# Quarter 0's head queries: behind quarter 2's keys and values instead of behind quarter 0's, from inputs kept in DRAM

## The chip, the core and the metric

One core of a Trainium2 chip runs the whole kernel. The metric is the device time in microseconds (us) of one execution, as the median of several runs. The engines are TensorE (PE; PEld are its weight loads), VectorE (DVE), ScalarE (ACT), GpSimd (POOL) and SyncE (SP, which issues most loads); each has its own queue of instructions, taken in order. ACT's queue also issues the stores.

## The reference

One decoder layer over 2048 tokens of width 1024, in float32: sparse attention with a top-256 indexer, then a SwiGLU network, each followed by a layer norm.

```
proj = h @ w_in                      # q | c_kv | q_idx | k_idx | w_idx
c_kv = rms_norm(c_kv, kv_norm_g)
q_lat = einsum('blhd,hcd->blhc', q, w_uk) * HEAD_DIM ** -0.5
rel   = relu(einsum('bqhd,bsd->bqhs', q_idx, k_idx))
score = einsum('bqh,bqhs->bqs', w_idx, rel)            # causal, else -inf
sel   = top_k(score, 256)
logits = einsum('bqhc,bqkc->bhqk', q_lat, c_kv[sel]) - slope * distance
o_lat  = einsum('bhqk,bqkc->bqhc', softmax(logits), c_kv[sel])
o = einsum('blhc,hcd->blhd', o_lat, w_uv) @ w_o
x = layer_norm(alpha * x + o);  x = layer_norm(alpha * x + swiglu_ffn(x))
```

The change touches only where `q`, the heads' part of the projection, is computed for the first 512 tokens.

## The kernel before

The tokens are worked on in four quarters of 512 (four blocks of 128 each). Until the attention starts, the program is a list of steps in `ORDER`, each a letter and a quarter:

- `i` (`index_part`, then `scores`): transposes the quarter of x on TensorE into 8 tiles of 128x512, each as a high and a low float32r part (tags `xh`, `xl`, `XB` = 8 buffers of each); projects index keys, index queries and the latent (the last matmuls are 264 columns wide); then computes the index scores of its blocks: per head two or more matmuls (L360), a ReLU on ACT (L362) and a weighted addition into the block's score row `S` on DVE (L365, L367).
- `k` (`kv_part`): keys and values of the quarter from the latent, stored to DRAM (`ks`, `vs`).
- `h` (`heads_part`): the heads' queries, eight tiles of 24 matmuls of 512 columns, one weight load and one split of it into two parts on POOL (L188, L159) for each; stored to DRAM as `qs`.
- `w` prepares the weights of `k`; `f` finishes the selection of blocks 2 to 7.

Every product of float32 values is three float32r matmuls (L234 to L236). Behind each `i` step stands the top-256 search of its blocks (`topk_near`): nine rounds in which a threshold is moved by a count, on DVE (L436 to L441) for two blocks and on ACT (L446 to L448) for the other two. It has a low priority: a scheduler, which orders each engine's instructions by priority and by its own model of time, puts it where it thinks there is room. `topk_rest` then reads one flag on DVE (L515 to L520) and branches at L521 (`tc.If`, an exact search that these inputs do not need). All engines take that branch, so it is a gate in every queue. There are two: one for blocks 2 to 7, one for blocks 8 to 15, the second called from the attention over the first 1024 tokens. Behind it `select` turns the scores into masks on DVE and ACT (L535 to L545).

`heads_part` takes its 8 pairs of input tiles either as they are left from the `i` step of its quarter (quarters 0 and 3 here), or loads them again from the DRAM tensor `xs`, to which `transposed` wrote them (`spill`, quarters 1 and 2 here). The attention follows the last `h` step: logits (L629), mask and row minimum on DVE (L630), exponentials on ACT (L635), transposes (L657) and their copies (L659), values (L668).

Of the kernel before, what the change touches and what calls it, by code (L numbers as in the profile page):

```python
# [46 lines left out]
XB = 8  # L47
# [3 lines left out]
NEV, NRL, NRAW = 3, 2, 2  # L51
NHI, NLO = 2, 2
NCS = 4
ORDER = "i0 w0 k0 h0 i1 k1 i2 f0 k2 i3 k3 h3 h2 h1".split()
ROUNDS = 9
BITS = {0: ([2], [3]), 1: ([4, 5], [6, 7]), 2: ([8, 9], [10, 11]), 3: ([12, 13], [14, 15])}

# [18 lines left out]
def trunk(tc, x, w_in, w_uk, w_uv, kv_g, w_o, w_gu, w_down, lm_g, lm_b, lf_g, lf_b, out, stop=99):  # L76
# [64 lines left out]
    xs = dram.tile([NQUART, KT, 2, P, QUART], F32, name="xs")  # L141
# [111 lines left out]
    def later():  # L253

        return at(tc.cur_priority + 1000000)
# [39 lines left out]
    def index_part(pp, pq, pe, bk, st, t):  # L295

        t0 = t * QUART
        tok = slice(t0, t0 + QUART)
        n0 = 8 if t == 1 else 12
        xx = transposed(pp, bk, "x", x, t0, XB, nat=[S[b] for b in range(n0, n0 + 4)], spill=xs[t] if t in (1, 2) else None)  # L300
        xh, xl = xx
        kst = st["kst"]

# [67 lines left out]
    def heads_part(pp, pe, bk, t, xx):  # L371

        t0 = t * QUART
        tok = slice(t0, t0 + QUART)
        if xx is None:
            xx = reloaded(pp, "x", xs[t], XB)
        for j in range(NPAIR):
            o = proj_tile(pp, bk, xx, [(lambda v: v, w3[:, :, j * P:(j + 1) * P])])
            evac(pe, o, 0.125, qs[j], tok)
# [781 lines left out]
    S = {}  # L1161
# [14 lines left out]
    with Banks("psb", big=(2, 2)) as big:  # L1176
        pe = pool("pe")
        pp = pool("pp")
        pq = pool("pq", "right")
        with Banks("psp", tp=(2, 1), mm=(2, 1)) as sml:  # L1180
            bk = lambda tag: big("big") if tag == "sc" else sml(tag)
# [3 lines left out]
            done = {}  # L1185
            for what, t in ((o[0], int(o[1])) for o in ORDER):
                if what == "i":
                    done[t] = index_part(pp, pq, pe, bk, st, t)
                    for b in range(max(2, t * BPQ), (t + 1) * BPQ):
                        scores(pq, bk, st, b)  # L1190
                    with later():
                        topk_near(tk, *BITS[t])
                elif what == "f":
                    with later():
                        topk_rest(tk, ((2, 2), (4, 4)))
                elif what == "w":
                    kv_weights()
                elif what == "k":
                    kv_part(pp, pe, bk, st, t)
                else:  # L1200
                    heads_part(pp, pe, bk, t, done[t] if t in (0, 3) else None)
        close("pq", "pp")
        ak = pool("ak", "right")
        ap = pool("ap", "right")
# [1 line left out]
        with Banks("psa", tp=(3, 1), oc=(1, 1)) as sml:  # L1206
            bk = lambda tag: big("big") if tag == "mm" else sml(tag)
# [61 lines left out]
```

## Time and profile before

| | us |
|---|---|
| median of 3 runs (lowest, highest) | 3155.91 (3154.04, 3174.88) |
| the profiled execution | 3164.37 |
| its span, first to last instruction | 3162.6 |
| TensorE busy in the span | 2963.8 |

In the trace, `mm`, `big`, `tp` and `oc` are tiles that TensorE writes, `wraw`, `whi` and `wlo` a weight and its two parts, `sm` a tile of logits or probabilities, `rl` the ReLU of scores. A busy time is the union of an engine's instructions. A wait is idle time of an engine, put down to what released it. A row "a <- b" of waits says that a waited for b.

### The profile page before, as it was taken

What the parts mean: (1) busy time and instruction counts of PE and PEld (TensorE: products, weight loads), DVE (VectorE), ACT (ScalarE), POOL (GpSimd) and SP (SyncE); (2) the same over time, 40 slices, a digit from 0 to 9 for tenths busy, and PEclk for the clock granted to TensorE, in tenths of its full rate; (3) what the DMA queues carried; (4) which work ended last, traced back from release to release, by engine and by line L of the source; (5) the groups of instructions that cost most, each with busy time, mean ns of one, the idle gap of its engine ahead of it and who ended that gap; (6) DMA issues with size and microseconds to landing.
All of it is one profiled execution on the core that took longest, in us unless ns stands there. A gap on an engine that the chain in (4) does not pass through costs nothing.

```text
span 3162.6 us, 44469 instructions
## 1 busy us (share of the span) xinstructions
PE 2963.8 (94%) x15067; PEld 2303.2 (73%) x15067; DVE 1918.4 (61%) x2904; ACT 1541.2 (49%) x2913; POOL 1557.1 (49%) x1342
## 2 busy tenths in 40 slices
PE   7988899887899999999999989999899999999996
PEld 5776677665566776676777768888678888878875
DVE  3436869977954544655556675555865555245299
ACT  2434858459877777666632233333333333333333
POOL 4433143452543334333336366666776666645475
PEclk9999999998899999999999979999899999999998
DMA  9777655573346756776559443223233222755353
GB/s 291 227 211 227 194 166 176 176 226 94 110 124 173 188 150 158 191 181 171 142 155 267 149 145 109 100 100 104 99 131 107 100 100 87 233 170 170 107 162 138
DMA packets 460728, 498.98 MB, mean 158 GB/s; under 512 B 51408, under 2 KB 332112, under 8 KB 460496
## 3 DMA queue, kind: packets, MB, share of 16 engines
q1 hardware_dynamic: 369280, 359.09, 40.4%
q10 hardware_dynamic: 91216, 137.01, 12.2%
q8 instruction: 120, 1.97, 0.3%
q14 instruction: 112, 0.92, 0.1%
HBM read 359.01 MB, written 136.97 MB: 157 GB/s over the span
## 4 chain that ended last, share of the span: by engine, by line
PE 63%; DVE 9%; DMA 4%; ACT 3%; issue 2%; SPq 1%; POOL 0%; ACTq 0%; DVEq 0%; POOLq 0%
PE mm L234 9%; PE mm L236 9%; PE mm L235 9%; PE oc L668 8%; PE tp L657 8%; PE big L629 7%; PE mm L1056 3%; PE mm L1054 3%; PE mm L1055 3%; DVE cl L159 1%; PE mm L837 1%; PE mm L838 1%; PE mm L839 1%; DVE hx L872 1%; DMA inv<-rsd 1%
## 5 line engine op out<-in xcount | busy, mean ns | idle before, releaser
L618 POOL TENSOR_SCALAR sm<-S 128x768 f32<-128x768 f32 (+7 forms) x384 | 339.7, 892 | 527.7 <-PE tp L657 473.9
L234 PE MATMUL mm<-ch,wh 128*128 128x512 f32 x1232 | 492.3, 401 | 16.5 <-ACT ch L867 13.6
L235 PE MATMUL mm<-cl,wh 128*128 128x512 f32 x1232 | 485.9, 395 | 6.6 <-DVE cl L159 5.7
L236 PE MATMUL mm<-ch,wl 128*128 128x512 f32 x1232 | 489.1, 397 | 0.0
L630 DVE CUSTOM_DVE_ANT_0 sm<-big,sm 128x1024 f32<-128x1024 f32 (+7 forms) x256 | 232.6, 922 | 247.6 <-PE big L629 203.2
L659 ACT COPY pt<-tp 128x512 f32<-128x512 f32 (+1 forms) x524 | 274.3, 559 | 181.3 <-PE tp L657 179.0
L635 ACT ACTIVATE sm<-sm,mx 128x768 f32<-128x768 f32 (+7 forms) x384 | 343.8, 899 | 23.9 <-DVE mx L630 23.5
L657 PE MATMUL tp<-ident,sm 128*128 128x128 f32 x2176 | 312.6, 284 | 27.5 <-ACT sm L635 17.2
L159 POOL TENSOR_TENSOR wl<-s,wh 128x512 fp32r<-128x512 f32 x176 | 238.4, 1360 | 194.9 <-ACT wh L920 194.9
L657 PEld LDWEIGHTS tp<-ident,sm 128*128 128x128 f32 x2176 | 236.5, 142 | 132.8 <-issue 97.5
L234 PEld LDWEIGHTS mm<-ch,wh 128*128 128x128 f32 x1232 | 235.3, 191 | 68.3 <-ACT ch L867 17.8
L235 PEld LDWEIGHTS mm<-cl,wh 128*128 128x128 f32 x1232 | 235.1, 191 | 64.0 <-DVE cl L159 9.8
L236 PEld LDWEIGHTS mm<-ch,wl 128*128 128x128 f32 x1232 | 235.4, 191 | 54.7
L920 ACT CAST wh<-s 128x512 fp32r<-128x512 f32 x176 | 109.0, 621 | 332.9 <-DVE s L909 91.4
L629 PE MATMUL big<-kka,aqd 128*128 128x512 f32 (+3 forms) x896 | 232.3, 387 | 25.2 <-DVE mx L630 19.6
L159 POOL TENSOR_TENSOR wl<-wr,wh 128x512 fp32r<-128x512 f32 x132 | 190.0, 1440 | 97.5 <-ACT wh L920 96.0
L159 POOL TENSOR_TENSOR cl<-hx,ch 128x512 fp32r<-128x512 f32 (+2 forms) x106 | 152.8, 1445 | 157.2 <-ACT ch L1049 136.2
L367 DVE SCALAR_TENSOR_TENSOR S<-rl,wi,S 128x768 f32<-128x768 f32 (+5 forms) x161 | 177.8, 1122 | 82.4 <-ACT rl L362 77.5
L668 PE MATMUL oc<-pt,vva 128*64 128x256 f32 (+1 forms) x1536 | 206.5, 390 | 0.8 <-DVE ot L672 0.8
L1049 ACT CAST ch<-hx 128x512 fp32r<-128x512 f32 (+2 forms) x158 | 94.8, 610 | 217.4 <-PE tp L1055 96.9
L362 ACT ACTIVATE rl<-big 128x768 f32<-128x768 f32 (+5 forms) x184 | 141.6, 790 | 118.5 <-PE big L360 57.2
L188 POOL TENSOR_SCALAR whi<-wraw 128x1024 fp32r<-128x1024 f32 (+1 forms) x60 | 72.6, 1211 | 253.8 <-PE mm L235 118.7
(296 smaller groups left out, 6556.1 us busy)
## 6 DMA issues: line engine op xcount, KB each, us to landing
wr<-in_f_w_gu SPq DMA_DIRECT2D x44, 1024.0 KB, 5.2
gs<-cc ACTq DMA_DIRECT2D x154, 256.0 KB, 2.0
hx<-gs SPq DMA_DIRECT2D x144, 256.0 KB, 2.9
aqd<-qs SPq DMA_DIRECT2D x256, 128.0 KB, 3.6
wraw<-in_a_w_in SPq DMA_DIRECT2D x56, 512.0 KB, 4.1
kka<-ks SPq DMA_DIRECT2D x96, 256.0 KB, 4.4
hx<-in_f_w_down SPq DMA_DIRECT2D x66, 256.0 KB, 3.0
qd<-qis SPq DMA_DIRECT2D x112, 128.0 KB, 4.5
```

The costliest lines, as they stand in the source:

```text
L159: (eng or nc.vector).tensor_tensor(out=lo, in0=src, in1=f(hi), op=ALU.subtract)
L234: nc.tensor.matmul(o, lhsT=lh, rhs=rh, start=(i == 0), stop=False)
L235: nc.tensor.matmul(o, lhsT=lh, rhs=rl, start=False, stop=False)
L236: nc.tensor.matmul(o, lhsT=ll, rhs=rh, start=False, stop=(i == n - 1))
L367: nc.vector.scalar_tensor_tensor(sv, rl[:, :wn], wi[:, h:h + 1], sv, op0=ALU.mult, op1=ALU.add)
L618: nc.gpsimd.tensor_scalar(out=sm[:, :wn], in0=S[b0 + i][:, w0:w0 + wn], scalar1=slope, scalar2=1.0, op0=ALU.mult, op1=ALU.mult)
L629: pe(nc.tensor.matmul(o[:, s0:s0 + n], lhsT=qd[:, c, i * P:(i + 1) * P], rhs=kk[wi_][e][:, s0:s0 + n], start=(c == 0), stop=(c == 1)))
L630: nc.vector.tensor_tensor_reduce(out=sm[:, :wn], in0=o, in1=sm[:, :wn], scale=-1.0, scalar=mx[:, i, 0:1] if wi_ else 3.0e38, op0=ALU.add, ...
L635: nc.scalar.activation(sm[:, :n], sm[:, :n], AF.Exp, bias=mx[:, i_, nw - 1:nw], scale=-1.0, accum_out=su[:, i_, e, w_:w_ + 1])
L657: pe(nc.tensor.transpose(tp[:, at:at + P], self.prob(e, i, kb), ident))
L659: pcopy(pt[:, :2 * n], tp[:, :2 * n])
L668: pe(nc.tensor.matmul(self.ob[e * HD:(e + 1) * HD, i0 * P:256], lhsT=self.vv[kb][:, e * HD:(e + 1) * HD], rhs=pt[:, e * n:(e + 1) * n], st ...
```

## The change

`h0` moves in `ORDER` from behind `k0` to behind `k2`. By then the input tiles of quarter 0 have been overwritten by those of quarters 1 and 2, so `transposed` now writes them to `xs` in `i0` as well, and `heads_part` loads them again.

```diff
@@ -51,7 +51,7 @@
 NEV, NRL, NRAW = 3, 2, 2
 NHI, NLO = 2, 2
 NCS = 4
-ORDER = "i0 w0 k0 h0 i1 k1 i2 f0 k2 i3 k3 h3 h2 h1".split()
+ORDER = "i0 w0 k0 i1 k1 i2 f0 k2 h0 i3 k3 h3 h2 h1".split()
 ROUNDS = 9
 BITS = {0: ([2], [3]), 1: ([4, 5], [6, 7]), 2: ([8, 9], [10, 11]), 3: ([12, 13], [14, 15])}
 
@@ -297,7 +297,7 @@
         t0 = t * QUART
         tok = slice(t0, t0 + QUART)
         n0 = 8 if t == 1 else 12
-        xx = transposed(pp, bk, "x", x, t0, XB, nat=[S[b] for b in range(n0, n0 + 4)], spill=xs[t] if t in (1, 2) else None)
+        xx = transposed(pp, bk, "x", x, t0, XB, nat=[S[b] for b in range(n0, n0 + 4)], spill=xs[t] if t < 3 else None)
         xh, xl = xx
         kst = st["kst"]
 
@@ -1198,7 +1198,7 @@
                 elif what == "k":
                     kv_part(pp, pe, bk, st, t)
                 else:
-                    heads_part(pp, pe, bk, t, done[t] if t in (0, 3) else None)
+                    heads_part(pp, pe, bk, t, done[t] if t == 3 else None)
         close("pq", "pp")
         ak = pool("ak", "right")
         ap = pool("ap", "right")
```

The scheduler lays out every engine's queue anew. At the start of ACT's queue, where the transposed tiles of quarter 0 are made (`xh`, `xl` their two parts, `S` here the staging for the weights of `w`, `kh` the index keys), stood before:

```order
L210 CAST xh<-tp 128x512 x8
L268 CAST S_171<-S_169 128x1024
L270 DMA wkv<-S_171 128x1024
L271 DMA wkv<-S_172 128x1024
L307 CAST kh<-mm 128x512
```

and stands now:

```order
L210 CAST xh<-tp 128x512 x2
L213 DMA xs<-xh 128x512 x2
L214 DMA xs<-xl 128x512 x2
L210 CAST xh<-tp 128x512 x2
L213 DMA xs<-xh 128x512 x2
L214 DMA xs<-xl 128x512 x2
L210 CAST xh<-tp 128x512
L213 DMA xs<-xh 128x512
```

Eight more such stores follow among the last casts and the first stores of `wkv`; they are new in this place.

On PE, right behind the last tile of `k0` (`cth`, `ctl` are the latent's two parts), stood the first tile of `h0`, on the tiles that `i0` left:

```order
L234 MATMUL mm_1130<-whi_1096,cth_503 128x512
L235 MATMUL mm_1130<-wlo_1097,cth_503 128x512
L236 MATMUL mm_1130<-whi_1096,ctl_504 128x512
L234 MATMUL mm_1146<-xh_234,whi_1141 128x512
L235 MATMUL mm_1146<-xl_235,whi_1141 128x512
```

Now `i1` follows there, and `h0` stands behind `k2`, on tiles that were loaded again (`xh_4482` and so on), with score matmuls of the third quarter's blocks between its own:

```order
L234 MATMUL mm_4578<-xh_4482,whi_4573 128x512
L235 MATMUL mm_4578<-xl_4483,whi_4573 128x512
L236 MATMUL mm_4578<-xh_4482,wlo_4574 128x512
L360 MATMUL big_3146<-kst_207,qd_3099 128x512 x2
L360 MATMUL big_3146<-kst_207,qd_3099 128x384 x2
L360 MATMUL big_3154<-kst_207,qd_3099 128x512 x2
L234 MATMUL mm_4578<-xh_4486,whi_4573 128x512
L235 MATMUL mm_4578<-xl_4487,whi_4573 128x512
```

On PE at the second gate (L521) stood before, with 252 matmuls of the attention ahead of it:

```order
L629 MATMUL big<-kka,aqd 128x512 x4
L668 MATMUL oc<-pt,vva 64x256 x2
L668 MATMUL oc<-pt,vva 64x128 x2
L657 MATMUL tp<-ident,sm 128x128 x4
L521 UNCONDITIONAL_BRANCH
L657 MATMUL tp<-ident,sm 128x128 x4
```

(the trace records each L668 as two, so that it has some 300 records there), and now, with 25:

```order
L236 MATMUL mm<-xh,wlo 128x512
L629 MATMUL big<-kka,aqd 128x128 x2
L629 MATMUL big<-kka,aqd 128x256 x2
L657 MATMUL tp<-ident,sm 128x128 x6
L629 MATMUL big<-kka,aqd 128x384 x2
L629 MATMUL big<-kka,aqd 128x512 x2
L629 MATMUL big<-kka,aqd 128x384 x2
L629 MATMUL big<-kka,aqd 128x512 x2
L657 MATMUL tp<-ident,sm 128x128 x3
L521 UNCONDITIONAL_BRANCH
```

The last head matmul (`mm<-xh,wlo`) now stands just ahead of the gate. Behind it both orders have the same attention. Counted the same way, 384 score matmuls stand ahead of the last 264-wide latent matmul of quarter 3, where 324 stood. From the end of quarter 3's latent projection to the second gate DVE has 50 score additions (62 before), 22 counts and 22 threshold steps of the search (36 and 36) and 8 mask-and-minimum pieces (30), ACT 60 ReLUs (75), 27 sign counts (36), 8 exponentials (30) and 2 copies of transposes (28).

## Rows read from the trace of the kernel before

**Rows 1.** The page's busy time by engine over the whole span.

```profile
PE 2963.8 (94%) x15067; PEld 2303.2 (73%) x15067; DVE 1918.4 (61%) x2904; ACT 1541.2 (49%) x2913; POOL 1557.1 (49%) x1342
```

**Rows 2.** Busy time by stage; last columns: granted clock, DMA share, GB/s.

```profile
0.00:79.00 79.00, 58.30 (x272) 46.18 (x272) 27.22 (x38) 20.72 (x41) 36.17 (x85) 0.92 1.00 291
79.00:114.00 35.00, 31.03 (x122) 23.00 (x122) 23.65 (x56) 19.88 (x44) 5.61 (x9) 0.93 0.82 250
114.00:158.00 44.00, 44.00 (x193) 36.01 (x192) 11.33 (x21) 14.24 (x34) 27.95 (x16) 1.00 0.68 209
290.00:395.00 105.00, 93.01 (x455) 74.92 (x454) 85.56 (x155) 76.24 (x168) 31.81 (x33) 0.95 0.60 179
395.00:447.00 52.00, 52.00 (x280) 45.00 (x279) 25.12 (x27) 19.31 (x34) 24.28 (x16) 1.00 0.54 148
704.00:784.00 80.00, 54.90 (x305) 37.56 (x304) 64.14 (x122) 75.33 (x151) 27.67 (x38) 0.83 0.30 87
1027.00:1185.00 158.00, 157.19 (x1130) 111.96 (x1131) 76.48 (x177) 121.02 (x265) 58.33 (x77) 1.00 0.64 169
447.00:784.00 337.00, 285.28 (x1288) 220.02 (x1286) 287.49 (x386) 239.11 (x412) 136.68 (x112) 0.94 0.56 171
```

**Rows 3.** Waits of TensorE, 704 to 784: total us, times, longest.

```profile
PE tp L657 <- ACT sm L635: 13.4, 10, 3.1
PE big L629 <- DVE mx L630: 5.8, 5, 1.7
```

**Rows 4.** Timeline of VectorE at the gate: start, duration in us.

```profile
780.30 0.14 DVE L519 TENSOR_SCALAR worsti<-all 1x1 int32<-1x1 f32 x1
784.15 1.09 DVE L630 CUSTOM_DVE_ANT_0 sm<-big,sm 128x896 f32<-128x896 f32 x1 [3.71 <-DVEq L521]
```

**Rows 5.** Line 234: durations in ns (min/median/max), first and last start.

```profile
L234 PE MATMUL mm<-whi,xh x128: 278/283/425, 53.6 to 446.4; 128*128 128x264 f32 x128
```

**Rows 6.** DMA issues, 0 to 1000 us: KB each, us to landing.

```profile
xs<-xh ACTq DMA_DIRECT2D x16, 256.0 KB, 4.7
xh<-xs SPq DMA_DIRECT2D x16, 256.0 KB, 5.1
```

**Rows 7.** Line 367, then timelines of VectorE and POOL near 590 us.

```profile
L367 DVE SCALAR_TENSOR_TENSOR S<-rl,wi,S x161: 474/1020/3418, 69.6 to 675.3; 128x768 f32<-128x768 f32 x42, 128x896 f32<-128x896 f32 x42, 128x1024 f32<-128x1024 f32 x28, 128x384 f32<-128x384 f32 x21
590.92 3.33 DVE L367 SCALAR_TENSOR_TENSOR S<-rl,wi,S 128x896 f32<-128x896 f32 x1
590.96 5.51 POOL L159 TENSOR_TENSOR wlo<-wraw,whi 128x1024 fp32r<-128x1024 f32 x2
```

**Rows 8.** Groups of ScalarE, 447 to 784: busy us, mean ns, idle.

```profile
L362 ACT ACTIVATE rl<-big 128x1024 f32<-128x1024 f32 (+2 forms) x76 | 69.5, 926 | 52.0 <-DVE S L367 13.4 <-PE big L360 10.3 <-PE mm L236 9.6
L446 ACT ACTIVATE ja<-S,t 128x1408 int8<-128x1408 f32 (+3 forms) x36 | 62.5, 1737 | 1.1 <-POOL t L423 1.1
L635 ACT ACTIVATE sm<-sm,mx 128x128 f32<-128x128 f32 (+7 forms) x30 | 23.0, 771 | 1.5 <-DVE mx L630 1.5
L659 ACT COPY pt<-tp 128x512 f32<-128x512 f32 (+1 forms) x28 | 14.3, 559 | 1.6 <-PE tp L657 1.4
```

**Rows 9.** Groups of VectorE, 447 to 784, in the same columns.

```profile
L367 DVE SCALAR_TENSOR_TENSOR S<-rl,wi,S 128x1024 f32<-128x1024 f32 (+2 forms) x68 | 92.6, 1379 | 22.6 <-ACT rl L362 19.3 <-DVEq L521 3.1
L436 DVE TENSOR_SCALAR_CACHE_REDUCE jv<-S,t 128x1152 int8<-128x1152 f32 (+3 forms) x36 | 62.6, 1740 | 2.7 <-POOL t L423 2.5
L630 DVE CUSTOM_DVE_ANT_0 sm<-big,sm 128x128 f32<-128x128 f32 (+7 forms) x30 | 20.9, 725 | 9.2 <-PE big L629 9.1
L441 DVE SCALAR_TENSOR_TENSOR t<-g,st,t 128x1 f32<-128x1 f32 x36 | 10.4, 329 | 0.4
```

**Rows 10.** Groups of TensorE, 690 to 784, the attention's three lines.

```profile
L629 PE MATMUL big<-kka,aqd 128*128 128x512 f32 (+3 forms) x96 | 26.3, 413 | 5.8 <-DVE mx L630 5.8
L657 PE MATMUL tp<-ident,sm 128*128 128x128 f32 x108 | 21.2, 324 | 19.3 <-ACT sm L635 13.4 <-ACT pt L659 5.7
L668 PE MATMUL oc<-pt,vva 128*64 128x256 f32 (+1 forms) x104 | 13.4, 381 | 0.0
```

## The prediction

> **What bounds the kernel now.** I read the page's head first, then the busy time by stage, then the waits of TensorE in the one stage that stands out, then the groups of instructions there. Over the span TensorE is busy 94% [rows 1], so most of the 3162.6 us is matmuls that this change only carries from one place to another. The stages [rows 2] show where time is lost. From 0 to 79 us the sixteen DMA engines are busy all of the time (share 1.00, 291 GB/s) and TensorE 58.3 of 79 us. From 114 to 158 TensorE is busy throughout: these are the 192 matmuls of step h0, the heads' queries of quarter 0. VectorE is busy 85.6 of 105 us between 290 and 395. The worst stage is 704 to 784: TensorE 54.9 of 80 us at a granted clock of 0.83, while ScalarE is busy 75.3 us. There the first pairs of the attention run beside the last top-k search, and TensorE waits for the exponentials and for the row minima [rows 3]. At the end of that stage stands the second gate, the branch at L521 that every engine takes when VectorE knows whether the last blocks need the exact search: VectorE reads the flag at 780.3 us and goes on at 784.15, after a wait of 3.71 us [rows 4]. I call 784 the time of the gate. After the attention has settled, TensorE is busy 157.2 of 158 us with 1130 matmul records, 0.140 us each [rows 2].
>
> So the change is worth what it does to two dates: when the gate opens, and how much attention stands before it.
>
> **The change part by part.** All dates are of the profiled execution. I carry them from the end of quarter 3's latent projection, whose last matmul starts at 446.4 us [rows 5], to the gate.
>
> Spill of quarter 0's transposed inputs: 16 DMAs of 256 KB, 4.19 MB, on ScalarE's queue among the casts of the first 30 us. Such a store lands after a median of 4.7 us where the kernel has them already [rows 6]. The place is the stage with DMA share 1.00. Bounds: nothing, if the loads that TensorE waits for overtake; 4.19 MB / 291 GB/s = 14.4 us, if all of it goes ahead of them. Nothing is idle on the DMA side, so I stay near the upper end: 12 us.
>
> h0 leaves 114 to 158: 192 matmuls at 44.0 us / 193 = 0.228 us [rows 2], about 44 us, and everything from i1 to k2 comes 44 us earlier. Quarter 1's own 32 DMAs for inputs and spill (4.19 MB of it stores) now fall into k0, where the share is 0.82 of 35 us, so 6 us are free and 8 of 14.4 us are not [rows 2]. Bounds 0 and 14.4; TensorE has other work in k0, so I take 4 us. That quarter 1's transposes no longer wait for h0's buffers, and quarter 3's now do, I set against each other at zero.
>
> h0 comes back behind k2: the same 44 us, so this pair cancels. The 16 reloads (4.19 MB, 5.1 us each to land [rows 6]) run while k2 computes, at a share of 0.54 to 0.60 [rows 2], and cost nothing; without that cover 14.4 us. SP's queue issues them between the weights and the queries of the scores, and each of the others there waits only behind issues. But h0 stands among the scores of blocks 8 to 11 now, on a VectorE that was 81% busy. Its eight weight splits run on POOL: 16 instructions, 27.95 us between 114 and 158 [rows 2], 3.5 us for a split. One score addition that began beside such splits took 3.33 us, where the median of all 161 is 1.02 [rows 7]. Low end nothing (TensorE has h0's own matmuls to do), high end 8 x 3.5 us = 28 us if each split held one addition for its whole length. The 68 additions of the later stretch, with as many splits beside them, took a mean of 1.379 us [rows 9], some 0.36 us over that median, so I take a microsecond for each split: 8 us.
>
> Here the Trainium skill speaks against the change: "SBUF — State Buffer", section "Who interferes with whom", says that a VectorE instruction with two inputs in SBUF contends with a GpSimd instruction that reads SBUF, and that whoever is second is blocked until the first is done. By that rule the term would be the 28 us of the high end, by the row's mean 8 us. The 3.33 us row agrees with the rule for one case.
>
> Scores ahead: in the new order 384 score matmuls stand ahead of the end of quarter 3's latent projection, in the old one 324. The 60 cost up to 0.228 us each, 13 us, and are gone from what follows.
>
> End of quarter 3's latent projection: 447 + 12 + 4 + 8 + 13 = 484 us.
>
> From there to the gate: 337 us in the trace, with VectorE busy 287.5 and ScalarE 239.1 of them [rows 2]. The new order has less in that piece, partly because scores and the search of blocks 8 to 11 ran earlier, partly because attention now comes after the gate. VectorE loses 12 score additions (1.379 us), 14 counts of the search (1.740), 14 threshold steps (0.329) and 22 mask-and-minimum pieces (0.725) [rows 9]: 16.5 + 24.4 + 4.6 + 16.0 = 61.5 us, so 226 remain, 0.786 of before. ScalarE loses 15 ReLUs (0.926), 9 sign counts (1.737), 22 exponentials (0.771) and 26 copies (0.559) [rows 8]: 13.9 + 15.6 + 17.0 + 14.5 = 61 us, so 178 remain, 0.745. At the same share of idle time the piece takes 265 us by VectorE and 251 by ScalarE; neither runs without the other, so I take 258. Bounds: 276, if no wait shrinks (337 - 61), and 251.
>
> Gate: 484 + 258 = 742 us, 42 earlier than 784.
>
> What that gives up: the old order has some 308 matmul records of attention ahead of the gate [rows 10], the new one 25. The 283 that now come later cost 283 x 0.140 = 39.6 us at the settled rate. The selection of blocks 8 to 15 on VectorE follows the gate in both orders and is taken as equal; everything behind is the same order, and TensorE carries a shift there to the end.
>
> Sum: 42 - 39.6 = 2.4 us gained. The profiled execution took 3164.4 us (span 3162.6), 8.5 over the median of the three runs, 3155.9; on that median the forecast is 3153 us, no change.
>
> **The rivals.**
> 1. *The seam empties out.* The stores and splits hide (12, 4 and 8 all zero) and the rest runs at ScalarE's 251 us: gate at 447 + 13 + 251 = 711, 73 earlier, gain 33 us, 3123 us. For it: ScalarE is the engine that was full from 704 to 784 [rows 2], and the search moves to where it idles. Against: the early stores enter a saturated stage. Chance 0.15.
> 2. *The gate holds up the attention.* It now stands 25 matmuls into the attention instead of 308, and TensorE takes its instructions in order: if the last search is late, TensorE stands before the gate with nothing to do. Each microsecond past 744 (784 less 39.6) is a loss. With 14.4 for the spill, 14.4 for k0 and 28 for the splits, quarter 3 ends at 517, and with 265 us more the gate opens at 782: 2 - 39.6 = 38 us lost, 3194 us. For it: all three ends have a row behind them. Against: VectorE then has less queued behind quarter 3. Chance 0.15.
> 3. *Every split blocks a score addition in full*, the rest as forecast: 20 us more, gate at 762, 18 us lost, 3173 us; by mechanism one step of rival 2, in size no change within 1%. One row shows it, the mean of 68 speaks against. Chance 0.15. This is the skill's rule just named.
>
> That the change does not do what it says is excluded by the new order itself.
>
> **How the numbers follow.** The forecast has 0.55. One per cent is 31.6 us, about what a measurement can tell from no change. Within 1%: forecast and rival 3, 0.70; faster 0.15, slower 0.15. The range goes from 3114, a little past rival 1, to 3190, which leaves out the far end of rival 2; the likeliest case alone spans 3135 to 3170.
>
> **What would show it.** Latent projection of quarter 3 ends near 484 us; the flag is read near 738; TensorE busy under 58 us in the first 79; hardly any attention ahead of the gate, and TensorE waiting less there than the 13.4 and 5.8 us of [rows 3]. A gate before 712 proves rival 1, one past 776 rival 2. Score additions of blocks 8 to 11 with a mean well over 1.4 us would show rival 3. The forecast is wrong if the stages before 450 us slip by much more than 37 us, or if the selection behind the gate costs more with the attention not yet under way.

## The result and the profile after

The change made the kernel slower: 3175.73 us, median of 20 runs (3166.97 to 3185.12), against 3158.75 (3149.93 to 3174.88) for 20 of the kernel before; ratio 1.0051, 95% interval 1.0041 to 1.0062, so some 16 us: half a per cent, clear of the noise. Forecast was a gain of 2.4 us. The profiled execution took 3167.53 us (span 3165.7).

The busy time over the span, beside [rows 1], shows nothing: TensorE does the same work.

```profile
PE 2961.7 (94%) x15067; PEld 2302.5 (73%) x15067; DVE 1930.6 (61%) x2904; ACT 1543.3 (49%) x2913; POOL 1556.8 (49%) x1342
```

The stages of the changed kernel, in the columns of [rows 2]: `i0`; `k0`; `h0` in its new place; `i3`; `h1`; the stretch before the second gate; the settled attention; and the piece from quarter 3's latent projection to the gate.

```profile
0.00:79.00 79.00, 56.57 (x256) 45.70 (x256) 19.60 (x27) 17.13 (x32) 32.35 (x79) 0.91 1.01 304
79.00:133.00 54.00, 40.81 (x161) 30.13 (x162) 32.09 (x78) 32.62 (x76) 8.11 (x15) 0.87 0.89 299
353.70:409.50 55.80, 55.80 (x249) 45.93 (x248) 24.17 (x29) 17.77 (x28) 30.57 (x18) 1.00 0.59 175
409.50:469.30 59.80, 55.60 (x310) 47.42 (x309) 52.29 (x70) 39.50 (x72) 25.56 (x23) 1.00 0.43 118
648.00:730.00 82.00, 69.22 (x276) 54.18 (x274) 66.35 (x86) 63.51 (x99) 39.46 (x28) 0.90 0.78 230
730.00:749.50 19.50, 11.56 (x35) 7.53 (x34) 14.80 (x32) 8.91 (x22) 13.98 (x18) 0.57 0.20 69
1027.00:1185.00 158.00, 156.96 (x1127) 111.48 (x1126) 75.77 (x175) 121.70 (x268) 60.75 (x80) 1.00 0.65 174
469.00:749.00 280.00, 235.85 (x959) 184.21 (x958) 239.30 (x284) 180.23 (x293) 119.80 (x85) 0.92 0.59 182
```

Two rows differ most from their counterparts. `k0` lasts 54 us where 35 stood, with TensorE idle for 13 of them and the DMA engines moving 299 GB/s where they moved 250. And the last piece before the gate is 280 us long, where the forecast has 258. TensorE's waits around the end of `h1` and the gate, beside [rows 3]:

```profile
PE big L629 <- DVE mx L630: 6.1, 5, 3.0
PE mm L234 <- DMA xh<-xs: 5.8, 1, 5.8
PE mm L234 <- DVE evl L284: 5.3, 1, 5.3
PE tp L657 <- ACT sm L635: 2.7, 3, 1.0
```

The second row is the reload of `h1`'s inputs: no score matmuls are left there to stand in for it. The flag, beside [rows 4], is read at 745.76, and the last such latent matmul, beside [rows 5], starts at 468.6 (its group of three ends at 469.2):

```profile
745.76 0.14 DVE L519 TENSOR_SCALAR worsti<-all 1x1 int32<-1x1 f32 x1
751.86 0.82 DVE L630 CUSTOM_DVE_ANT_0 sm<-big,sm 128x640 f32<-128x640 f32 x1 [5.96 <-PE tp L657]
```
```profile
L234 PE MATMUL mm<-whi,xh x128: 280/283/425, 61.2 to 468.6; 128*128 128x264 f32 x128
```

**Against which profile.** The two first profiles differ by 3 us only, the medians by 17. A second profile of the kernel before shows where they part:

> The kernel before as it is, for a second profile of it: its one profiled run took 3164, 7 us above the median of its runs (3157), while the changed kernel's two took 3166 and 3168, 8 to 10 below its own (3176), so the two profiles differ by 3 us where the medians differ by 17. Theory that the whole 17 us lie up to the first quarter of the attention, and the first profile of before was a late one there: the 280th of the attention's score instructions (L629; 924.2 us in the first profile, 930.2 in the changed kernel) comes at 914 to 919. Theory that the two stand 5 to 6 us apart there and the rest is spread of what follows: at 922 to 926 again, with a shorter rest.

It took 3156.89. Its `k1` ends at 277.3 us, as in two other kernels with the same order up to there (275.8, 277.1); the first profile had it at 288.0 and kept these 10 us as far as the attention. The 280th score instruction of the attention (L629, counted from 0) starts at 918.6 there. Three profiles of the changed kernel have it at 930.2, 930.6 and 934.4, so 12 to 16 of the 16 us lie before it. Behind it the two kernels run alike to a few us (the attention ends 12 to 19 us later in the three). All dates of "before" from here on are of this second profile:

```profile
0.00:111.70 111.70, 89.73 (x393) 70.20 (x394) 52.27 (x96) 40.78 (x86) 41.19 (x94) 0.91 0.94 284
384.50:436.40 51.90, 51.90 (x279) 44.94 (x278) 28.59 (x28) 19.85 (x36) 24.36 (x16) 1.00 0.54 151
436.40:772.30 335.90, 287.98 (x1264) 222.43 (x1263) 285.15 (x386) 237.13 (x408) 136.85 (x112) 0.92 0.54 169
772.30:918.60 146.30, 123.52 (x804) 86.10 (x802) 113.21 (x185) 114.14 (x243) 74.99 (x64) 0.92 0.40 118
```

They are: the start up to the end of `k0`; from the end of `k2` to that of `i3`'s projections; from there to the flag; from the flag to the 280th score instruction. The same stretches of the changed kernel, `h0` and `i3` together in the second row:

```profile
0.00:133.10 133.10, 97.48 (x417) 75.94 (x418) 51.69 (x104) 49.84 (x107) 40.47 (x94) 0.90 0.96 302
353.60:469.20 115.60, 111.40 (x557) 93.35 (x556) 76.46 (x99) 57.27 (x99) 56.07 (x40) 1.00 0.51 146
469.20:745.80 276.60, 232.58 (x945) 181.15 (x943) 239.00 (x284) 180.14 (x293) 119.60 (x85) 0.92 0.59 183
745.80:930.20 184.40, 159.45 (x1060) 112.10 (x1060) 130.44 (x234) 142.48 (x308) 85.44 (x84) 0.94 0.42 120
```

### The profile page after: what moved, and what is told of

Same layout as the page of the kernel before. It is cut to its first block, busy times and chain, and to the rows that moved or that the text cites. A ratio compares the mean times of both kernels' runs of the same rounds, so it can differ in the third digit from the quotient of the medians.

```text
span 3165.7 us, 44529 instructions
## 1 busy us (share of the span) xinstructions
PE 2961.7 (94%) x15067; PEld 2302.5 (73%) x15067; DVE 1930.6 (61%) x2904; ACT 1543.3 (49%) x2913; POOL 1556.8 (49%) x1342
## 4 chain that ended last, share of the span: by engine, by line
PE 62%; DVE 7%; DMA 3%; issue 2%; ACT 1%; SPq 1%; POOL 1%; DVEq 0%; ACTq 0%; POOLq 0%
PE mm L235 8%; PE mm L236 8%; PE mm L234 8%; PE tp L657 8%; PE oc L668 8%; PE big L629 8%; PE mm L1056 2%; PE mm L1054 2%; PE mm L1055 2%; DVE cl L159 1%; PE mm L837 1%; PE mm L838 1%; PE mm L839 1%; DVE hx L872 1%; PE tp L1056 1%
## 5 line engine op out<-in xcount | busy, mean ns | idle before, releaser
L159 POOL TENSOR_TENSOR wl<-s,wh 128x512 fp32r<-128x512 f32 x176 | 239.5, 1366 | 194.6 <-ACT wh L920 194.6
L657 PE MATMUL tp<-ident,sm 128*128 128x128 f32 x2176 | 309.7, 283 | 13.4 <-ACT sm L635 7.0
L629 PE MATMUL big<-kka,aqd 128*128 128x512 f32 (+3 forms) x896 | 229.5, 384 | 26.0 <-DVE mx L630 19.9
L367 DVE SCALAR_TENSOR_TENSOR S<-rl,wi,S 128x768 f32<-128x768 f32 (+5 forms) x161 | 188.5, 1189 | 88.5 <-ACT rl L362 86.7
L159 POOL TENSOR_TENSOR wl<-wr,wh 128x512 fp32r<-128x512 f32 x132 | 190.3, 1443 | 95.6 <-ACT wh L920 94.1
L159 POOL TENSOR_TENSOR cl<-hx,ch 128x512 fp32r<-128x512 f32 (+2 forms) x106 | 152.9, 1446 | 154.9 <-ACT ch L1049 135.9
L668 PE MATMUL oc<-pt,vva 128*64 128x256 f32 (+1 forms) x1536 | 205.6, 388 | 0.6 <-DVE ot L672 0.6
```

The source lines that it names most:

```text
L159: (eng or nc.vector).tensor_tensor(out=lo, in0=src, in1=f(hi), op=ALU.subtract)
L367: nc.vector.scalar_tensor_tensor(sv, rl[:, :wn], wi[:, h:h + 1], sv, op0=ALU.mult, op1=ALU.add)
L629: pe(nc.tensor.matmul(o[:, s0:s0 + n], lhsT=qd[:, c, i * P:(i + 1) * P], rhs=kk[wi_][e][:, s0:s0 + n], start=(c == 0), stop=(c == 1)))
L657: pe(nc.tensor.transpose(tp[:, at:at + P], self.prob(e, i, kb), ident))
L668: pe(nc.tensor.matmul(self.ob[e * HD:(e + 1) * HD, i0 * P:256], lhsT=self.vv[kb][:, e * HD:(e + 1) * HD], rhs=pt[:, e * n:(e + 1) * n], st ...
```

## The experiments

Theory of the start: the loss is made in the first 133 us, by stores of transposed inputs that now fall where the DMA engines are full, and by `h0` no longer standing between `k0` and quarter 1's stores. Theory of the gate: the loss is made at the second gate, which holds up the attention. For every kernel the table gives its ratio to the kernel before, timed beside it, with its interval, and from its profile the end of `k0`, for some the MB moved until then (GB/s times us), and the dates of the flag and of the 280th score instruction.

| kernel | ratio (95%) | k0 ends | MB | flag | 280th |
|---|---|---|---|---|---|
| before | 1 | 111.7 | 31.7 | 772.3 | 918.6 |
| changed | 1.0051 (1.0041, 1.0062) | 133.1 | 40.2 | 745.8 | 930.2 |
| e1 before, stores of quarter 0 too | 1.0066 (1.0048, 1.0085) | 120.9 | 36.0 | 793.9 | 937.3 |
| e2 changed, no trip for quarter 0 | 1.0088 (1.0068, 1.0109) | 127.6 | | 756.3 | 939.9 |
| e3 changed, gate later | 1.0082 (1.0063, 1.0100) | 133.5 | | 797.7 | 938.5 |
| e6 before, gate first | 1.0111 (1.0090, 1.0132) | 109.3 | 31.8 | 742.7 | 948.4 |
| e7 before, h1 behind k2 | 1.0020 (1.0004, 1.0036) | 110.9 | | 785.1 | 922.0 |
| e8 changed, h0 behind k1 | 1.0064 (1.0041, 1.0086) | 131.6 | 40.3 | 804.0 | 935.9 |
| e9 changed, no stores 0 and 1 | 0.9987 (0.9972, 1.0001) | 110.6 | 31.7 | 732.1 | 919.8 |
| e10 changed, no stores 1 | 1.0036 (1.0021, 1.0050) | 122.4 | 36.1 | 727.8 | 917.0 |
| e13 changed, no stores 0 | 1.0061 (1.0048, 1.0074) | 127.3 | 36.4 | 747.6 | 938.9 |
| e14 changed | 1.0051 (1.0039, 1.0064) | 132.2 | 39.9 | 748.8 | 934.4 |
| e11 changed, stores late | 1.0081 (1.0064, 1.0097) | 136.5 | 40.7 | 751.9 | 937.2 |
| e12 before, h2 behind k2 | 1.0021 (1.0007, 1.0035) | 113.8 | | 790.2 | 923.0 |
| e15 before, h1 behind k1 | 1.0012 (1.0001, 1.0023) | 110.5 | | 827.7 | 915.9 |
| e16 changed, stores by SyncE | 1.0074 (1.0055, 1.0094) | 130.4 | | 755.7 | 946.0 |
| e17 changed, stores by GpSimd | 1.0117 (1.0098, 1.0136) | 133.7 | | 767.4 | 958.7 |
| e18 before, stores by SyncE | 0.9998 (0.9986, 1.0011) | 110.0 | 31.8 | 774.8 | 920.2 |

**e1: the stores alone.** To the kernel before:

```diff
-        xx = transposed(..., spill=xs[t] if t in (1, 2) else None)
+        xx = transposed(..., spill=xs[t] if t < 3 else None)
```

> The kernel before, in which the first quarter's transposed inputs are also stored to DRAM; nobody reads them back, and the heads' queries of the first quarter stay where they were, on the tiles in SBUF. Theory of the start (the 16 stores in the full DMA queues of the first 79 us, and what they push into the step behind, last to the end): 9 to 17 us slower than before, so 3168 to 3176, with quarter 0's latent projection ending some 10 us after the 68.2 us of before and a delay of about that size still there at the start of the attention. Theory of the gate (the loss is made where the last search ends, not at the start): within 4 us of before, 3155 to 3163, the delay of the start eaten by later idle time.

3178.45 against 3156.83: 21 us, as much as the whole change. `i0` ends 9.6 us later, and at the attention's start it is 21. The theory of the start holds; the size is over its upper end. The scheduler also laid out the steps behind anew, and the delay grows there (9.2 us at the end of `k0`, 17.1 at that of `i3`'s projections); whether the new layout makes the surplus was not tested.

**e2: the move without the trip.** To the changed kernel:

```diff
-        xx = transposed(..., spill=xs[t] if t < 3 else None)
+        xx = transposed(..., spill=xs[t] if t in (1, 2) else None)
-            xx = reloaded(pp, "x", xs[t], XB)
+            xx = reloaded(pp, "x", xs[t], XB) if t else transposed(pp, bk, "x", x, t0, XB, nat=[S[b] for b in range(12, 16)])
```

> The changed order without the trip through DRAM: quarter 0's inputs are not stored, and the first quarter's heads, at their new place, load x again and transpose it again (32 transposes, 8 copies, 8 subtractions more; 16 stores of 256 KB and 16 loads of 256 KB fewer, 8 loads of 256 KB more). Theory of the start: the stores go, so 9 to 17 us of the loss go, 3159 to 3167 against the changed kernel's 3176. Theory of the gate: the gate stands at the same place, ahead of the same attention, so 3174 to 3182 (4 us of transposes more, some of the start's delay less).

3184.36: the range of the theory of the start is missed by far, that of the gate by 2 us. `i0` ends at 66.3 again, yet `k0` at 127.6. So quarter 0's stores are not all there is in the start: quarter 1's now fall there too.

**e3: the gate later.** To the changed kernel, in the flag's chain of `topk_rest` (`b0 == 8` is the second gate), and at the place of its call among the pairs of heads:

```diff
-        nc.vector.tensor_scalar(out=ge, in0=above[:, b0:b1], scalar1=float(TOPK - 8), ...)
+        nc.vector.tensor_scalar(out=dep, in0=(sums[0][:, 5, 3:4] if b0 == 8 else one), scalar1=0.0, scalar2=float(TOPK - 8), op0=ALU.mult, op1=ALU.add)
+        nc.vector.tensor_scalar(out=ge, in0=above[:, b0:b1], scalar1=dep, ...)
...
-    REST = 2
+    REST = 7
```

> The changed kernel with the gate put later: the flag's first addition now reads a sum that the third group of the second pair of heads writes, so that the scheduler puts 270 of the attention's TensorE instructions ahead of the gate, where the changed kernel has 25 and the kernel before 252; nothing else is changed. Theory of the gate: the last search takes about 9 us longer with attention beside it (107 us against 98 in the two traces), and 245 instructions at 0.14 us, 34 us, are done in the meantime: the attention ends about 20 us earlier than in the changed kernel, 3150 to 3160 against its 3176, so no slower than the kernel before. Theory of the start: the gate's place does not matter, because the work that waits for it is limited by VectorE and ScalarE either way; 3171 to 3181.

3180.6: the theory of the gate, in this form, falls. Beside the search the attention hardly advances: its 60th score instruction comes at 777.5 us, 5 earlier than in the changed kernel, while the flag, which now waits for the attention, moves by 52, and the selection behind it with it.

**e6: the price of the gate.** To the kernel before, behind the second flag, an addition to the first block of scores that changes nothing but the order:

```diff
         nc.vector.tensor_scalar(out=wi_, in0=all_, ...)
+        b0 == 8 and nc.vector.scalar_tensor_tensor(S[0][0:1, 0:1], all_, 0.0, S[0][0:1, 0:1], op0=ALU.mult, op1=ALU.add)
-                attention(ak, ap, None, bk, 0, 1024, 1024, EARLY[0], {REST: rest})
+                rest(); attention(ak, ap, None, bk, 0, 1024, 1024, EARLY[0])
```

> The kernel before with the gate put ahead of the whole attention: after the flag is read, one addition writes to the first block of scores, so that no score of the attention can be made ahead of it; TensorE has 4 attention instructions ahead of the gate where before has 252, and up to the start of the attention the two programs are the same, instruction by instruction. The prediction's price (the search runs 9 us shorter without attention beside it, and 248 instructions at 0.140 us, 34.7, go behind the gate): 26 us slower, 3183. Theory that VectorE's and ScalarE's work up to the selection's end sets the time and the attention ahead of the gate only fills gaps that come back later: 3152 to 3166, with the 280th score instruction of the attention at 915 to 929.

3192.18, 35 us (28 to 42) slower. The program is the same up to there, so this is the gate alone: the flag comes 29.6 us earlier, the 280th score instruction 29.8 later. TensorE's column (first) in the stretch before the flag and behind it:

```profile
660.60:742.70 82.10, 28.68 (x124) 22.46 (x122) 67.91 (x93) 62.56 (x95) 16.59 (x16) 0.72 0.35 100
742.70:948.40 205.70, 171.90 (x1081) 121.10 (x1081) 135.86 (x251) 150.05 (x326) 82.12 (x102) 0.87 0.38 111
```

TensorE works 28.7 of 82.1 us before the flag. The prediction's kind of price for attention behind the gate is right, and a gate with almost none ahead is dearer than its rate: the stretch behind the flag is 59.4 us longer (205.7 against 146.3), where the rate gave 34.7. The theory that the attention ahead of the gate only fills gaps falls.

**e7, e8: other places.** Of the kernel before (e7) and of the changed one (e8):

```diff
-ORDER = "i0 w0 k0 h0 i1 k1 i2 f0 k2 i3 k3 h3 h2 h1".split()
+ORDER = "i0 w0 k0 h0 i1 k1 i2 f0 k2 h1 i3 k3 h3 h2".split()
...
-ORDER = "i0 w0 k0 i1 k1 i2 f0 k2 h0 i3 k3 h3 h2 h1".split()
+ORDER = "i0 w0 k0 i1 k1 h0 i2 f0 k2 i3 k3 h3 h2 h1".split()
```

> The kernel before with the heads' queries of the second quarter, instead of the first, behind the third quarter's keys and values (k0 h0 stay together; h1's inputs make their trip through DRAM as they do before): the late move without anything new at the start. Theory that taking h0 from behind k0 makes the loss (TensorE's waits in k0 uncovered, 12 us late there): nothing of it here, 3150 to 3160. Theory that a block of projections behind k2 is what costs (it carries scores ahead, and the gate then comes before the attention has got far): 3166 to 3180.

> The changed kernel with the first quarter's heads one step earlier, behind the second quarter's keys and values: the same stores and loads, the same hole behind k0, another place of the 192 matmuls. Theory that the hole behind k0 and the stores make the loss: the same 12 us late at the end of k0, and 3170 to 3182. Theory that the place behind k2 makes it: 3155 to 3166.

e7: 3163.62. A late block of projections with nothing new at the start costs 6 us (1 to 11), between the two ranges. e8: 3178.64. `h0` one step earlier than in the changed kernel, with the same start, costs 20, as the theory of the start has it.

**e4, and e9, e10, e13, e14: the stores taken out of the changed kernel.** e9 is

```diff
-        xx = transposed(..., spill=xs[t] if t < 3 else None)
+        xx = transposed(..., spill=xs[t] if t == 2 else None)
-            xx = reloaded(pp, "x", xs[t], XB)
+            xx = reloaded(pp, "x", xs[2], XB)
```

and e10 and e13 likewise, with `t in (0, 2)`, where quarter 1 reads `xs[0]`, and `t in (1, 2)`, where quarter 0 reads `xs[1]`. Left out is the right input of those quarters' queries; loads and matmuls are as many as before. e4 and e14 are the changed kernel as it is.

> The changed kernel as it is, for a second profile of it: the one profiled run took 3168, the median of 20 is 3176 and their spread is 18 us. If the 8 us are in the stages up to the end of the attention (1590 us in the profile), a second profile shows them there, and the theory of the start or of the gate has to carry them; if they are in what follows, which the change does not touch, the attention ends at 1590 again and the rest differs.

> The changed kernel without the stores of the first two quarters' transposed inputs: h0 and h1 load the third quarter's stored inputs in their place (as many loads, at the same time), so that the part of the computation left out is the queries' right input; order and matmuls are the changed kernel's. Theory of the start's bytes (in the changed kernel the DMA engines are full until k0 ends at 133 us, 40 MB at 302 GB/s, in the kernel before 32 MB until 112): 8.4 MB fewer, so k0 ends at 112 to 119, set by TensorE, and with the start's loss gone the move alone is neutral: 3154 to 3163. Theory that the new place costs (h0 among the scores, gate ahead of the attention): 3168 to 3176, however early k0 ends.

> The changed kernel without the stores of the second quarter's transposed inputs alone (h1 loads the first quarter's, as many loads; the queries' right input is the part left out). These stores are in the kernel before too, but there they come behind h0, after 158 us; the change brings them into k0. Theory of the start's bytes: 4.2 MB fewer before the end of k0, 4.2/0.302 = 14 us: k0 ends at 119 to 123 with i0 still 10 us late, total 3162 to 3170. Theory that only the first quarter's stores count: k0 at 130 to 133, 3172 to 3180.

> The changed kernel without the stores of the first quarter's transposed inputs alone (h0 loads the second quarter's, as many loads; the queries' right input is the part left out). Theory of the start's bytes: i0 ends at 65 to 68 us, k0 at 119 to 125, and the total lies between the 3152 without both and the 3176 with both: 3160 to 3168, so that the two sets of stores add up. Theory that one of the two sets makes the whole loss: within 4 of 3152 or of 3176.

> The changed kernel as it is, with timed runs. Its two profiles (3168, 3166) are the lowest of its runs. Theory that the start and the gate carry the whole difference of the medians: a run near 3176 has the 280th score instruction of the attention at 936 to 942 us instead of 930. Theory that the stages up to there cost 12 us and the rest is spread of what follows: at 928 to 933 whatever the total.

e9 decides between the stores and the new place: without these 32 stores the changed order takes 3151.64 us against 3154.21, no slower (and `k0`'s end and the time lie a little under the expected ranges). Its stretches, as above:

```profile
0.00:110.60 110.60, 89.51 (x417) 71.08 (x418) 51.69 (x91) 41.30 (x84) 41.99 (x94) 0.94 0.95 287
335.10:449.40 114.30, 111.09 (x558) 93.35 (x557) 75.14 (x98) 57.18 (x98) 55.78 (x40) 1.00 0.51 147
449.40:732.10 282.70, 234.87 (x945) 183.28 (x943) 241.82 (x283) 180.54 (x293) 118.91 (x85) 0.91 0.58 179
732.10:919.80 187.70, 159.93 (x1060) 113.08 (x1060) 131.68 (x235) 142.10 (x309) 80.17 (x84) 0.93 0.41 118
```

The DMA share up to the end of `k0` is 0.93 to 0.99 wherever the table gives the MB, and the date goes with the bytes: 32 MB by 109 to 112 us, 36 by 121 to 127, 40 by 132 to 137. Quarter 0's stores alone (e10) cost 11 us (7 to 16). But quarter 1's alone (e13, 3174.55) cost 19 (15 to 23), no less than both: the two do not add up, against what was expected.

The bytes are not all of it. The engines stay full (share 1.01 in the 6 to 10 us before) until 102 us in e9, 110 in e13 and 120 in the changed kernel, so that date moves with each set. What differs too is the rest of `k0` behind that date; e9, the changed kernel and e13:

```profile
102.00:110.60 8.60, 7.54 (x32) 5.78 (x32) 6.93 (x23) 6.68 (x17) 4.46 (x7) 1.00 0.51 168
120.00:133.10 13.10, 10.40 (x35) 7.40 (x34) 3.51 (x16) 11.51 (x32) 3.44 (x2) 0.80 0.39 132
110.00:127.30 17.30, 10.42 (x31) 7.86 (x32) 5.69 (x22) 14.39 (x40) 3.42 (x2) 0.70 0.33 111
```

In `k0` TensorE waits 8.7 us for ScalarE's copies of the values (`ve`) in e13, 6.1 in the changed kernel, 1.1 in e9 and 1.8 in e10. ScalarE's own timeline in e13, with its queue's DMA issues (ACTq), shows what stands ahead of these copies:

```profile
102.16 0.33 ACTq L286 DMA_DIRECT2D ks<-evl  x1
104.04 0.33 ACTq L214 DMA_DIRECT2D xs<-xl  x1
105.82 0.33 ACTq L286 DMA_DIRECT2D ks<-evl  x1
106.19 0.72 ACT L446 ACTIVATE ja<-S,t 128x512 int8<-128x512 f32 x1 [4.03 <-DMA ks<-evl]
107.66 0.56 ACT L400 COPY ve<-mm 128x512 f32<-128x512 f32 x1
108.13 0.72 ACT L446 ACTIVATE ja<-S,t 128x512 int8<-128x512 f32 x1
```

ScalarE stands 4.03 us among issues of stores, and then runs sign counts of a search between the copies that TensorE waits for. Up to the end of `k0` it has 9 of these counts (L446) in e13 and 8 in the changed kernel, 4 in e9 and e10: with other stores the scheduler laid out this queue in another way. So part of the loss at the end of `k0` comes through ScalarE's queue and not through the bytes; no run holds its order fixed, and how much is not shown.

e4 took 3165.75 and e14 3171.26 (profile 3173.2). In e14 the 280th score instruction comes at 934.4, 4 us later than in the other two, partly ahead of the flag (748.8) and partly behind it: neither of its two theories is borne out alone, and the last few us between the profiles and the medians are not placed.

**e11: the same bytes later.** To the changed kernel:

```diff
-        xx = transposed(..., spill=xs[t] if t < 3 else None)
+        xx = transposed(..., spill=xs[t] if t in (1, 2) else None)
                     done[t] = index_part(pp, pq, pe, bk, st, t)
+                    [store.dma_start(out=xs[0][kt, c], in_=f(done[0][c][kt])) for kt in range(KT) for c in range(2) if t == 0]
```

> The changed kernel with the first quarter's 16 stores issued behind the whole of i0 instead of tile by tile between its transposes; the same bytes, not among the first loads. Theory of the start's bytes: i0 ends early again (66 to 69 us), but the stores fall into k0 and k0 ends at 129 to 136 all the same: 3170 to 3181. Theory of the stores' place in the queue: i0 at 66 to 69 and k0 at 120 to 125: 3160 to 3169.

3181.33, `k0` at 136.5: moving the stores away from the first loads does not help. That `i0` would end at 66 to 69 was a miss (75.0). As in e13, TensorE waits 8.7 us for `ve`, so this end of `k0` is not set by the bytes alone either.

**e12, e15: one trip fewer in the kernel before.** To the kernel before (e12; in e15 likewise `h1` behind `k1`, and only quarter 2 is stored):

```diff
-ORDER = "i0 w0 k0 h0 i1 k1 i2 f0 k2 i3 k3 h3 h2 h1".split()
+ORDER = "i0 w0 k0 h0 i1 k1 i2 f0 k2 h2 i3 k3 h3 h1".split()
-        xx = transposed(..., spill=xs[t] if t in (1, 2) else None)
+        xx = transposed(..., spill=xs[t] if t == 1 else None)
-                    heads_part(pp, pe, bk, t, done[t] if t in (0, 3) else None)
+                    heads_part(pp, pe, bk, t, done[t] if t != 1 else None)
```

> The kernel before with the third quarter's heads directly behind its keys and values, on the inputs still in SBUF: no trip through DRAM for that quarter, 16 stores and 16 loads of 256 KB fewer between 280 and 560 us, where the DMA engines are busy 0.54 to 0.60 of the time; the start is that of before. Theory that bytes only cost where the DMA engines are full: nothing gained from the trip, and the late block of projections costs the few us it cost with h1 (3158 to 3168). Theory that the trip costs wherever it is: 3140 to 3152.

> The kernel before with the second quarter's heads directly behind its keys and values, on the inputs still in SBUF: its 16 stores and 16 loads are gone, between 158 and 290 us (DMA engines busy 0.76 of the time) and from 560 us on. Only two steps of heads stand behind the third quarter's part, so the attention comes earlier and more of it ahead of the gate (514 of its instructions on TensorE, before 252). Theory of the start's bytes: no gain from the trip, since the engines are not full there, and a gate that is late by what the attention takes from the search: 3158 to 3175. Theory that a trip costs wherever it is: 3138 to 3150.

3163.23 and 3158.61, by the ratios 7 and 4 us slower than before: 8.4 MB less buys no time where the engines are not full; e12 has the ratio of e7, which keeps the trip.

**e16, e17, e18: another queue.** In `transposed`, of the changed kernel (e16, and e17 with `nc.gpsimd`) and of the kernel before (e18):

```diff
-                store.dma_start(out=spill[kt, 0], in_=f(hi))
-                store.dma_start(out=spill[kt, 1], in_=f(lo))
+                nc.sync.dma_start(out=spill[kt, 0], in_=f(hi))
+                nc.sync.dma_start(out=spill[kt, 1], in_=f(lo))
```

> The changed kernel with all stores of transposed inputs issued by SyncE, which issues the loads, in place of ScalarE; the same bytes in the same places of the order. Theory of the start's bytes: 3168 to 3180, k0 ends at 130 to 136. Theory that ScalarE's issuing costs (its copies for TensorE wait behind issues that wait): k0 ends at 120 to 127, 3158 to 3167. A third way: SyncE's queue stands at a store until its tile is made, and the loads behind it come late: i0 later than 78, over 3180.

> The changed kernel with the same stores issued by GpSimd. Theory of the start's bytes: 3168 to 3180, k0 ends at 130 to 136. Theory that ScalarE's issuing costs: k0 at 120 to 127, 3158 to 3167. A third way: GpSimd splits the weights, and a store that it has to wait for or to prepare delays a split that TensorE needs: over 3180.

> The kernel before with its two quarters' stores issued by SyncE in place of ScalarE. If ScalarE's issuing costs, a few us of it are in the kernel before too: 3146 to 3153, a version that beats both. If only the bytes count, and these stores fall where the DMA engines are 0.6 to 0.8 busy: 3153 to 3160.

None helps. e16 takes 3182.5, with `k0` at 130.4, as for the bytes, and the total 2.5 us over their range; e17 3197.94, the third way; e18 3160.11 against 3160.17. So that ScalarE issues the stores is not what the changed kernel pays for; its sign counts between the copies stay in e16 (8 of them). The Trainium skill, "DMA: Bandwidth & Descriptors", section "Issuing engines are not separate DMA queues", says that all queues share the same 16 engines; e16 and e18 agree. With the stores on GpSimd's queue (e17) TensorE waits for the weights' splits up to 134 us (2.0 us in the changed kernel):

```profile
PE mm L234 <- POOL whi L188: 7.2, 2, 5.7
PE mm L236 <- POOL wlo L159: 6.4, 2, 5.2
```

No kernel tried is faster than the kernel before by more than its interval.

## Why the prediction was wrong, step by step

- **What bounds the start: right.** The DMA engines were named as full up to 79 us; in the changed kernel they are full up to 120.
- **Spill 12 us and k0 4 us: right in sum, by luck in the parts.** `i0` ends at 78.0 against 67.2 (74.1 in two other profiles: 7 to 11 us). `k0` ends 21.4 later; its row now holds 32 transposes of `i1` (5.1 us, 1.2 before), so 17.5 against 16. At the end of `k2`, with `h0`'s 44.3 us taken off, 13.4 are left (353.6 against 384.5 - 44.3). But there e9 is 5.1 us earlier than the kernel before (335.1), where the forecast set the order's own effect at zero; quarter 0's stores add 9.2 (e10, 344.3), quarter 1's another 9.3, more than twice the 4.
- **Score additions beside splits 8 us, scores ahead 13: right in sum.** From the end of `k2` to that of `i3`, 115.6 us against 51.9 + 44.3 = 96.2: 19.4 against 21. In e9 it is 18.1. TensorE's score matmuls take 13.3 us more there (27.7 against 14.4); 24 transposes of quarter 3 that now wait for `h0`'s buffers take 3.6, which the forecast set off against others at zero. TensorE is idle for 4.2 us only, none of it in `h0` and 2.3 of it for a split weight, so the 8 us for additions held up by splits are not there. Nor are the 28 us that the Trainium skill's rule ("SBUF — State Buffer", "Who interferes with whom") would have made of the splits alone: the additions of this stretch have a mean of 1.222 us, under the 1.4 that was to show it, since only 6 of the 30 begin during a split.

```profile
L367 DVE SCALAR_TENSOR_TENSOR S<-rl,wi,S 128x768 f32<-128x768 f32 (+2 forms) x30 | 35.5, 1222 | 29.2 <-ACT rl L362 29.2
```

- **End of quarter 3's latent projection, 37 us later: right**, 469.2 against 436.4, so 32.8.
- **"From there to the gate ... so I take 258": wrong; this is the step that failed.** Measured up to the flag, the piece shrank from 335.9 to 276.6 us, by 59; the forecast has it shrink by 79. VectorE was to lose 61.5 us of work and lost 46 (285.2 to 239.0). The counts of what leaves were nearly right, their prices not. The groups, beside [rows 9] and, for ScalarE's sign counts, [rows 8]:

```profile
L367 DVE SCALAR_TENSOR_TENSOR S<-rl,wi,S 128x896 f32<-128x896 f32 (+2 forms) x56 | 86.4, 1557 | 16.6 <-ACT rl L362 16.4
L436 DVE TENSOR_SCALAR_CACHE_REDUCE jv<-S,t 128x1664 int8<-128x1664 f32 (+3 forms) x25 | 46.5, 1861 | 1.2 <-POOL t L423 0.9
L446 ACT ACTIVATE ja<-S,t 128x1920 int8<-128x1920 f32 (+3 forms) x27 | 48.7, 1804 | 1.6 <-POOL t L423 1.6
```

  The means of mixed groups were the wrong price. Of the counts 11 left, not 14, six of 1152 columns and five of 1280, at 1.40 and 1.54 us and not 1.740: 16.1 us, where 24.4 were taken off. The 12 additions that left had 768 columns, 1.01 us each and not 1.379: 12 us, where 16.5 were taken off. And 5 of these came back, because the 21 additions of 1024 columns that stayed became slower. The second profile of the kernel before, then the changed kernel:

```profile
L367 DVE SCALAR_TENSOR_TENSOR S<-rl,wi,S 128x1024 f32<-128x1024 f32 x21 | 38.5, 1846 | 15.6 <-ACT rl L362 15.6
L367 DVE SCALAR_TENSOR_TENSOR S<-rl,wi,S 128x768 f32<-128x768 f32 x19 | 18.9, 1011 | 3.2 <-ACT rl L362 3.1
L367 DVE SCALAR_TENSOR_TENSOR S<-rl,wi,S 128x1024 f32<-128x1024 f32 x21 | 43.9, 2110 | 12.7 <-ACT rl L362 12.7
L367 DVE SCALAR_TENSOR_TENSOR S<-rl,wi,S 128x768 f32<-128x768 f32 x7 | 7.1, 1014 | 0.0
```

  What slows them is GpSimd's split of a weight. In the changed kernel, an addition that begins during a split, and one with no split beside it:

```profile
582.00 2.39 POOL L159 TENSOR_TENSOR wlo<-wraw,whi 128x1024 fp32r<-128x1024 f32 x1 [2.90 <-PE mm L236]
582.07 3.41 DVE L367 SCALAR_TENSOR_TENSOR S<-rl,wi,S 128x1024 f32<-128x1024 f32 x1
619.15 1.28 DVE L367 SCALAR_TENSOR_TENSOR S<-rl,wi,S 128x1024 f32<-128x1024 f32 x1 [0.34 <-ACT rl L362]
```

  The first ends 1.1 us after the split does, and so do the six others of 1024 columns that begin during one. Of the 21, 11 run beside such a split in each of the three profiles of the changed kernel and in e9, 7 in both of the kernel before. So the forecast put the splits' cost beside `h0` and left it out here, where it grew. All additions together shrink by 9.1 us (6.2 against the first profile).

  ScalarE lost 57 of the forecast's 61. And the middle between VectorE's 265 and ScalarE's 251 was the wrong choice: VectorE is the fuller engine, with a busy share of 0.85 before and 0.86 now. 239.0 us at 0.85 is 281, near the 276.6 measured; the piece came out at the bound of 276 that the prediction called "if no wait shrinks", and over it in the prediction's own terms (280, from 469 to 749).
- **So the gate: 26.5 us earlier, not 42** (59.3 - 32.8). That is less than the 39.6 at which rival 2 puts the break-even: its mechanism, at a smaller size.
- **Attention behind the gate, 39.6 us: right.** From the flag to the 280th score instruction 184.4 us against 146.3: 38.1. In e9, 41.4.
- **Sum.** 38.1 - 26.5 = 11.6 us lost at the 280th score instruction, 12 to 16 over three profiles, against 2.4 gained. In e9, without the start's stores, the gate is 40.2 us earlier and 41.4 are given back: the move by itself is worth nothing. The stores of the start, priced about right in sum, were to be paid for by a shorter last piece that did not come.
- **The rivals.** The seam did not empty out. The splits did not hold up every addition, though that rival's 3173 us lies nearest to the median, which is luck: its 20 us were to fall beside `h0`, and most of the additions that a split catches stand in the last piece. The time is inside the range, 3114 to 3190, and the loss inside the 1% that had 0.70; the forecast's sign was wrong.

## What to carry to other kernels

Add up the bytes to the point where the DMA engines stop being full, with everything that a move brings ahead of that point: work that moves no bytes is cover there, and taking it away costs as much as adding stores (e13 and e1, some 20 us each). Work that leaves a stage is priced by the shapes that leave, not by the mean of a mixed group; what stays can get dearer by what it now runs beside; and the idle share of the fuller engine is kept until something shows that it shrinks. Take the base of a sum from more than one profile: here one stage of one profile was 10 us late and hid most of the loss.

## What the runs showed of the hardware

- A VectorE addition of two inputs that begins while GpSimd splits a weight (L159) is held until the split is done: 1024 columns take 1.28 us alone, and 3.41 when they begin 0.07 us after a split of 2.39.
- Sets of stores in a full stretch move the date at which the DMA engines stop being full (102 us in e9 without both sets, 110 in e13 with one, 120 in the changed kernel with both), but do not add up in the kernel's time: the 16 stores of quarter 1 cost as much by themselves as with the 16 of quarter 0 (e13 19 us, the changed kernel 16). The engines' queues were laid out anew each time.
- The same stores from GpSimd's queue cost 21 us more than from ScalarE's (1.0117 and 1.0051 to the kernel before). The rows show TensorE waiting for GpSimd's splits.
